# Transfers of adaLN rows two steps ahead of their products, through four buffers instead of two

## The chip, the cores and the metric

The kernel runs on one core of a Trainium2 chip. The metric is the time of one execution on the device in microseconds (us). Weights lie in the chip's main memory in 32-bit floats and are brought to the core by DMA, all of them started from one instruction queue, SyncE's (SP below). The matrix engine (PE), the vector engine (DVE), the scalar engine (ACT) and GpSimd (POOL) each work through a list of instructions of their own, in an order that is fixed when the kernel is built, and wait for one another by semaphores.

## What is computed

Two layers of a decoder trunk for 256 tokens of width 1024. A conditioning vector `c` gives six vectors per layer (shift, scale and gate of two sub-layers) by a product with a 1024 x 6144 matrix:

```python
c_act = jax.nn.silu(c)
for l in range(DEPTH):
    mod = c_act @ w_mod[l] + b_mod[l]
    sh1, sc1, g1, sh2, sc2, g2 = jnp.split(mod, 6, axis=-1)
    h = modulate(rms_norm(x, mix_norm_g[l]), sh1, sc1)
    y = token_mixer(h, ...)          # MLA, MoBA and a 31-tap convolution branch, gated and merged
    x = x + g1[:, None, :] * y
    h = modulate(rms_norm(x, ffn_norm_g[l]), sh2, sc2)
    x = x + g2[:, None, :] * channel_mixer(h, ...)
```

The change touches only how `mod` is made inside the token mixers.

## The kernel before

**Weights.** Every weight matrix comes as units of 128 x 1024 numbers (512 KB). `wload` (line 193) starts a transfer into a `raw` tile (four buffers); `split` (line 206) makes a high part `whi` with ACT (line 213) and the rest `wlo` with DVE (line 215), four buffers each; PE multiplies the activations by both (lines 291, 292 and 294). `take` keeps three units (`AHEAD`) split ahead of use.

**adaLN rows.** Part of `mod` is made on PE (`mod_part`, line 389) and part on DVE. On DVE, one step brings 128 x 1024 numbers of the transposed matrix (`in_wmr`, 512 KB), multiplies them by the broadcast row silu(c) (`crow`) and sums along the row in one instruction (`use_row`, line 372, the "row product" below; a short read of the sum comes with it), and a one-column addition of the bias follows (line 373). Each step gives one column of `mod`. In the token mixer of layer 0 there are 16 such steps (parts 3 and 4, eight each), in that of layer 1 there are 8 (part 2, the gate g1). `step "R"` (line 1185) does transfer and product in one step, by `mod_row`, with the buffers of the tag `qkT`, of which there are two. Sixteen more row products run in the channel mixer of layer 0, through other buffers (line 1252).

**The row silu(c).** The steps `RW` (`row_load`, line 1172) load `c` into a tile of the tag `kv` (two buffers), take its tanh with ACT into a tile of `qkT` (line 1181) and finish `crow` on DVE (line 1182). The other users of these tags in a mixer are earlier: `qkT` holds queries and keys of the two attentions, `kv` the keys and values of MLA, `vb` (one buffer, line 881) the values of MoBA, last read by PE in line 668.

**Order.** `CFG["order"]` lists each mixer's steps in the order in which they are written out; R steps are spread between the steps `r0` and `r1`. What an engine really does in which order is decided once, at build time, by the framework's scheduler: it walks through its own estimate of time and gives each engine, whenever the engine is free there, the ready instruction that was written first. A tile is given a buffer of its tag when one is free by the same estimate, and the instruction waits in place on the chip if that turns out too early. A row product can so stand far ahead of its place in the list, and short instructions that were written much later (the tables `ta` and `tb` of the next layer, line 487; the gain `gs` of the channel mixer, line 571) stand wherever nothing written earlier was ready.

**Around the rows in the mixers.** DVE also runs the convolution taps (line 1061), the gating of the attention output (`out_ab`, line 1121, which frees a PSUM bank of the tag `psb`, three in all), and the convolution's normalisation (lines 1071 to 1100): its sum of squares goes through DVE (line 497), POOL (line 498) and PE (line 527).

Of the kernel before, what the change touches and what calls it, by code (L numbers as in the profile page):

```python
# [9 lines left out]
F32 = mybir.dt.float32  # L10
# [7 lines left out]
P = 128  # L18
S = 256
NB = 2  # L20
# [22 lines left out]
CDMA = 1  # L43
# [11 lines left out]
LINE = 512  # L55
# [6 lines left out]
ROWS = [(0, 0), (0, 1), (1, 0), (1, 1)] + RPARTS  # L62
# [40 lines left out]
def _order(l):  # L103
    o = []
    for w in STEPS[l].split():
        name = w.rstrip("0123456789")
        o.append((name, *(int(d) for d in w[len(name):])))
    o = _spread(o, [("V", j, t, min(31, t + TAPS)) for j in range(4) for t in range(0, 31, TAPS)], ("v", 0), ("v", 1))
    if ("r", 0) in o:
        o = _spread(o, [("R", r, k) for n, r in RPARTS if n == l for k in range(KD)], ("r", 0), ("r", 1))  # L110
    o = _spread(o, [("M",)] * (9 * len(PARTS[l])), ("m", 0), ("m", 1))
    return [t for t in o if t[0].isupper() and not (l == 0 and C0K and t[:2] == ("C", 0))]


CFG = {"order": [_order(0), _order(1)]}
# [35 lines left out]
def trunk_kernel(ctx, tc, xT, crow, ccol, pos, invf, modb_d, cols_d, grow_d, wmh, wmr, wm, win1, wqkv,  # L151
# [6 lines left out]
    wk = ctx.enter_context(tc.tile_pool(name="wk", bufs=2))  # L158
# [4 lines left out]
    def nm(s):  # L163
        uid[0] += 1
        return f"{s}_{uid[0]}"
# [7 lines left out]
    def e1():  # L173
        return wk.tile([P, S], F32, tag="e1", name=nm("e1"), bufs=8)
# [14 lines left out]
    def small(n, tag="sm", bufs=12):  # L189
        return wk.tile([P, n], F32, tag=tag, name=nm(tag), bufs=bufs)  # L190


    def wload(src, tag="raw", bufs=4):
        n = src.shape[1]
        t = wk.tile([P, 1024], F32, tag=tag, name=nm("raw"), bufs=bufs, align_bytes=LINE if tag != "raw" else None)
        sy.dma_start(t[:, 0:n], src)
        return t[:, 0:n]


    SPARE = ("oah", "oal", "obh", "obl")  # L200
# [164 lines left out]
    mod = [per.tile([P, 48], F32, name=f"mod{l}") for l in range(L)]  # L365

    def wload_row(l, r, k, tag=None):
        return wload(wmr[ROWS.index((l, r)), k], tag or SPARE[(2 * k + r) % 4], 2 if tag else 1)

    def use_row(raw, row, l, r, k, scale):  # L370
        acc = small(1, "m0", 4)
        ve.scalar_tensor_tensor(raw, raw, scale, row, op0=ALU.mult, op1=ALU.mult, accum_out=acc)  # L372
        return ve.tensor_tensor(mod[l][:, r * 8 + k:r * 8 + k + 1], acc, modb[:, l, r * 8 + k:r * 8 + k + 1],
                                op=ALU.add)

    def mod_row(row, l, r, k, tag=None, scale=1.0):

        return use_row(wload_row(l, r, k, tag), row, l, r, k, scale)
# [53 lines left out]
    def step(gen, n=1):  # L432
        for _ in range(n):
            next(gen, None)
# [241 lines left out]
    crow1 = []  # L676
# [22 lines left out]
    def layer(l):  # L699
# [4 lines left out]
        if l == 0:  # L704
# [26 lines left out]
            def prepare_tile(k):  # L731
                n = 1 if k < 4 else 2
                raws0 = [wload_row(0, r, k) for r in range(n)]
                accs = small(2, "m0", 4)
                for r in range(n):
                    ve.scalar_tensor_tensor(raws0[r], raws0[r], 1.0, crow0[0], op0=ALU.mult, op1=ALU.mult,
                                            accum_out=accs[:, r:r + 1])
                mods0.append(ve.tensor_tensor(mod[0][:, 0:16].rearrange("p (r k) -> p k r", r=2)[:, k, 0:n],
                                              accs[:, 0:n],
                                              modb[:, 0, 0:16].rearrange("p (r k) -> p k r", r=2)[:, k, 0:n], op=ALU.add))  # L740
                if k >= 4:
                    g = small(1, "gs", 12)
                    ve.scalar_tensor_tensor(g, mod[0][:, 8 + k:9 + k], 1.0, cv(l, "mix_g")[:, k:k + 1],
                                            op0=ALU.add, op1=ALU.mult)
                    gains.append(g)
                with tc.issue_after(mods0[-1].ins) if k else ExitStack():
                    ve.tensor_tensor(xn[k // 4][:, k % 4, :], x[:, k, :], bcs, op=ALU.mult)
# [56 lines left out]
        for k in range(KD):  # L804
# [4 lines left out]
            t = e1()  # L809
# [68 lines left out]


        qks = [None, None]  # L880
        vb = wk.tile([P, NB, 512], F32, tag="vb", name=nm("vb"), bufs=1)

        pqkv = {}

# [274 lines left out]
        def attend(fn, g):  # L1159
            if (fn, g) not in attns:  # L1160
                attns[fn, g] = fn(g)
            step(attns[fn, g])

        run = {
            "KL": latents, "LE": lat_evac, "GLU": glu, "LR": lat_rstd, "LT": lat_T, "QKV": proj_qkv, "UQ": up_q, "UK": up_kv,
            "MS": mla_rstd, "MP": mla_prep, "BS": moba_rstd, "BP": moba_prep, "MA": lambda g, p: attend(mla_attn, g), "BA": lambda g, p: attend(moba_attn, g), "C": gate_c, "V": conv,
            "LN": conv_mean, "LS": conv_rstd, "LB": conv_silu, "G": gate_ab, "O": out_ab, "OC": out_c, "PR": project, "M": lambda: step(mods),
        }
# [13 lines left out]
                ve.scalar_tensor_tensor(crow1[0], th, 1.0, crow1[0], op0=ALU.add, op1=ALU.mult)  # L1182

        run["RW"] = row_load
        run["R"] = lambda r, k: mod_row(crow1[0], l, r, k, "qkT", 0.5 if CDMA else 1.0)
        for tok in CFG["order"][l]:
            run[tok[0]](*tok[1:])
        step(mods, 99)
# [87 lines left out]
    for l in range(L):  # L1276
        layer(l)
# [86 lines left out]
```

## Time and profile before

| | us |
|---|---|
| median of 3 runs | 927.59 (927.27 to 927.75) |
| the profiled execution, whole | 925.46 |
| its span in the trace | 923.2 |
| PE busy | 894.6 |
| DVE busy | 789.0 |
| ACT busy | 554.3 |
| row products on DVE (line 372), 40 | 48.7 |
| DVE idle before row products, for their DMA | 3.4 |

The span is what the trace covers; 2.3 us of the execution lie around it. An engine is busy while one of its instructions runs; matmuls overlap, so PE's busy time is not PE at its peak. "Idle before X, until Y" is the time in which an engine stood still ahead of instruction X, and Y is what ended the wait.

### The profile page before, as it was taken

The numbers are of one execution on the slowest core, as the hardware profiler recorded it, in microseconds if no ns is written. First come the engines' busy times: TensorE is split into PE (matmuls) and PEld (weight loads), VectorE is DVE, ScalarE is ACT, GpSimd is POOL, SyncE is SP. The second block draws the span as 40 slices with busy tenths as digits, with TensorE's granted clock in tenths as the row PEclk, the third lists the DMA queues.
The fourth block names the chain that finished last, engine by engine and source line by source line (L and its number), as shares of the span: only waits on it lengthen the run. The fifth ranks groups of instructions, "written<-read, shape, count | busy, mean of one in ns | idle before, by whom it ended". The sixth has DMA issues, their size and how long they took to land.

```text
span 923.2 us, 18669 instructions
## 1 busy us (share of the span) xinstructions
PE 894.6 (97%) x7327; PEld 839.7 (91%) x7327; DVE 789.0 (85%) x1530; ACT 554.3 (60%) x980; POOL 43.4 (5%) x32
## 2 busy tenths in 40 slices
PE   6999989989999999999999999999999999999998
PEld 5988878989997999999979988789999899999998
DVE  6989899999987899988964999999777798777774
ACT  4677588734754655566643675976465566556561
POOL 0011500000000000000000042000000000000000
PEclk7999999999998999999999999999999999999999
DMA  8956534599877788876743665538757766666641
GB/s 316 390 193 207 170 103 159 182 316 321 293 259 250 265 277 281 309 229 222 227 155 106 206 217 181 195 119 274 239 173 244 259 214 221 194 194 194 196 138 46
DMA packets 57975, 201.59 MB, mean 218 GB/s; under 512 B 6944, under 2 KB 8480, under 8 KB 57888
## 3 DMA queue, kind: packets, MB, share of 16 engines
q1 hardware_dynamic: 57888, 200.41, 65.2%
q8 instruction: 57, 0.93, 0.4%
q14 instruction: 30, 0.25, 0.1%
HBM read 199.33 MB, written 1.05 MB: 217 GB/s over the span
## 4 chain that ended last, share of the span: by engine, by line
PE 77%; DVE 10%; DMA 6%; ACT 3%; issue 2%; POOL 2%; SPq 0%; POOLq 0%; DVEq 0%; ACTq 0%
PE psb L291 15%; PE psb L292 15%; PE psb L294 15%; PE psa L292 7%; PE psa L291 7%; PE psa L294 7%; DVE wlo L215 3%; DMA raw<-in_wmr 2%; POOL rs L498 2%; PE psa L389 2%; DMA raw<-in_wup 1%; DVE cacc L1061 1%; PE psa L668 1%; PE psa L656 1%; DMA raw<-in_wmh 1%
## 5 line engine op out<-in xcount | busy, mean ns | idle before, releaser
L213 ACT ACTIVATE whi<-raw 128x1024 fp32r<-128x1024 f32 (+2 forms) x286 | 295.8, 1041 | 210.9 <-PE psb L292 86.5
L215 DVE TENSOR_TENSOR wlo<-raw,whi 128x1024 fp32r<-128x1024 f32 (+2 forms) x286 | 340.0, 1194 | 74.2 <-ACT whi L213 61.0
L291 PE MATMUL psb<-hh,whi 128*128 128x256 f32 x1088 | 261.2, 281 | 1.3 <-ACT thc L782 1.3
L292 PE MATMUL psb<-hl,whi 128*128 128x256 f32 x1088 | 258.3, 279 | 0.0
L291 PEld LDWEIGHTS psb<-hh,whi 128*128 128x128 f32 x1088 | 204.7, 188 | 8.3 <-issue 4.0
L292 PEld LDWEIGHTS psb<-hl,whi 128*128 128x128 f32 x1088 | 204.4, 188 | 1.2 <-DVE hl L565 0.5
L294 PE MATMUL psb<-hh,wlo 128*128 128x256 f32 x1088 | 148.5, 278 | 0.0
L294 PEld LDWEIGHTS psb<-hh,wlo 128*128 128x128 f32 x1088 | 135.0, 188 | 0.8 <-issue 0.8
L1061 DVE SCALAR_TENSOR_TENSOR cacc<-upad,cw,cacc 128x256 f32<-128x256 f32 x240 | 104.3, 476 | 0.1
L292 PE MATMUL psa<-mhl,whi 128*128 128x256 f32 x400 | 93.5, 277 | 0.2 <-DVE mhl L1143 0.2
L291 PE MATMUL psa<-mhl,whi 128*128 128x256 f32 x400 | 93.6, 277 | 0.0
L1240 DVE SCALAR_TENSOR_TENSOR e<-psb,fw,e 128x255 f32<-128x255 f32 (+1 forms) x176 | 83.7, 477 | 10.3 <-ACT e L1238 9.2
L292 PEld LDWEIGHTS psa<-mhl,whi 128*128 128x128 f32 x400 | 74.9, 188 | 0.4 <-DVE mhl L1143 0.4
L291 PEld LDWEIGHTS psa<-mhl,whi 128*128 128x128 f32 x400 | 74.9, 188 | 0.0
L498 POOL TENSOR_TENSOR rs<-rs,mhalf 128x16 f32<-128x16 f32 (+3 forms) x22 | 41.8, 1908 | 687.7 <-DVE rs L497 686.9
L1238 ACT ACTIVATE e<-psb,fb,fw 128x256 f32<-128x256 f32 x88 | 48.7, 553 | 28.1 <-DVE e L1240 15.8
L294 PE MATMUL psa<-mhl,wlo 128*128 128x256 f32 x400 | 53.6, 277 | 0.0
L372 DVE SCALAR_TENSOR_TENSOR raw<-raw,crow 128x1024 f32<-128x1024 f32 x40 | 48.7, 1218 | 3.6 <-DMA raw<-in_wmr 3.4
L294 PEld LDWEIGHTS psa<-mhl,wlo 128*128 128x128 f32 x400 | 49.2, 188 | 0.0
L291 PE MATMUL psb<-whi,hh 128*128 128x416 f32 (+1 forms) x96 | 31.7, 354 | 3.9 <-ACT hh L811 3.9
L1248 ACT ACTIVATE mhl<-e 128x256 fp32r<-128x256 f32 x44 | 18.3, 416 | 26.6 <-DVE e L1246 24.6
L389 PE MATMUL psa<-raw,cact 128*32 128x256 f32 x320 | 31.9, 432 | 0.6 <-DMA raw<-in_wm 0.6
(272 smaller groups left out, 1472.2 us busy)
## 6 DMA issues: line engine op xcount, KB each, us to landing
raw<-in_wup SPq DMA_DIRECT2D x88, 512.0 KB, 4.6
raw<-in_wmr SPq DMA_DIRECT2D x52, 512.0 KB, 5.2
raw<-in_wdn SPq DMA_DIRECT2D x44, 512.0 KB, 4.4
raw<-in_wm SPq DMA_DIRECT2D x40, 512.0 KB, 4.4
raw<-in_wgab SPq DMA_DIRECT2D x32, 512.0 KB, 4.9
raw<-in_wqkv SPq DMA_DIRECT2D x24, 512.0 KB, 4.8
raw<-in_win SPq DMA_DIRECT2D x16, 512.0 KB, 4.6
raw<-in_wgc SPq DMA_DIRECT2D x16, 512.0 KB, 4.4
```

The costliest lines, as they stand in the source:

```text
L213: ac.activation(hi, raw, AF.Copy)
L215: ve.tensor_tensor(lo, raw, hi.bitcast(F32), op=ALU.subtract)
L291: te.matmul(o, p1[0], p1[1], start=start, stop=False)
L292: te.matmul(o, p2[0], p2[1], start=False, stop=False)
L294: te.matmul(o, p3[0], p3[1], start=False, stop=stop)
L372: ve.scalar_tensor_tensor(raw, raw, scale, row, op0=ALU.mult, op1=ALU.mult, accum_out=acc)
L389: te.matmul(acc[32 * c:32 * c + 32, 0:S], cact[:, k:k + 1].to_broadcast([P, 32]), raw[:, c * S:(c + 1) * S], start=(k == 0), stop=(k == KD ...
L498: gp.tensor_tensor(r, r, mhalf[:, :n], op=ALU.pow)
L1061: ve.scalar_tensor_tensor(aj, upad[:, j, t:t + S], cw[:, j * 31 + t:j * 31 + t + 1], aj, op0=ALU.mult, op1=ALU.add)
L1238: ac.activation(t, src, AF.Identity, scale=fw[:, 2, c:c + 1], bias=fb[:, c:c + 1])
L1240: ve.scalar_tensor_tensor(t[:, d:S], src[:, 0:S - d], fw[:, 2 - d, c:c + 1], t[:, d:S], op0=ALU.mult, op1=ALU.add)
L1248: ac.activation(mh, th, AF.Copy)
```

## The change

A row step no longer starts its own transfer. The first R step of a mixer starts the transfers of rows 0, 1 and 2, and each later one that of the row two ahead of it, as long as there are any. Row n goes to a buffer of the tag `qkT`, `vb`, `qkT` or `kv`, in turn. The tile `vb` is now aligned to 512 bytes, as the other three are. The products, their number and the order of the steps in the list stay as they were, and so do the row products of the channel mixer.

```diff
     def wload_row(l, r, k, tag=None):
-        return wload(wmr[ROWS.index((l, r)), k], tag or SPARE[(2 * k + r) % 4], 2 if tag else 1)
+        return wload(wmr[ROWS.index((l, r)), k], *(tag or (SPARE[(2 * k + r) % 4], 1)))
...
-        vb = wk.tile([P, NB, 512], F32, tag="vb", name=nm("vb"), bufs=1)
+        vb = wk.tile([P, NB, 512], F32, tag="vb", name=nm("vb"), bufs=1, align_bytes=LINE)
...
-        run["R"] = lambda r, k: mod_row(crow1[0], l, r, k, "qkT", 0.5 if CDMA else 1.0)
+
+        coming_rows = [t[1:] for t in CFG["order"][l] if t[0] == "R"]
+        fetched = []
+
+        def fetch_row():
+            if coming_rows:
+                n = len(fetched)
+                fetched.append(wload_row(l, *coming_rows.pop(0), (("qkT", 2), ("vb", 1), ("qkT", 2), ("kv", 2))[n % 4]))
+
+        used = [0]
+
+        def row_step(r, k):
+            for _ in range(1 if fetched else 3):
+                fetch_row()
+            use_row(fetched[used[0]], crow1[0], l, r, k, 0.5 if CDMA else 1.0)
+            used[0] += 1
+
+        run["R"] = row_step
```

## Rows read from the trace of the kernel before

**Rows 1.** The page's first part: busy us, share of span, instructions.

```profile
PE 894.6 (97%) x7327; PEld 839.7 (91%) x7327; DVE 789.0 (85%) x1530; ACT 554.3 (60%) x980; POOL 43.4 (5%) x32
```

**Rows 2.** Busy us (instructions) per engine, PE clock, DMA share, GB/s; both row stretches.

```profile
181.00:262.00 81.00, 77.13 (x666) 74.34 (x659) 77.12 (x156) 41.18 (x61) 0.77 (x1) 1.00 0.90 312
...
614.00:657.00 43.00, 42.08 (x379) 40.77 (x377) 41.88 (x79) 28.02 (x55) 0.00 (x0) 1.00 0.75 255
```

**Rows 3.** Waits of the whole span: who waited for whom, us, times, longest.

```profile
DVE raw L372 <- DMA raw<-in_wmr: 3.4, 4, 1.6
...
SPq L196 <- DVE raw L372: 32.9, 21, 3.4
...
SPq L196 <- PE psa L601: 6.7, 1, 6.7
```

**Rows 4.** SP's timeline, layer 0's row transfers: start us, us, line, what.

```profile
156.77 0.33 SPq L196 DMA_DIRECT2D raw<-in_wmr  x1
...
184.72 0.33 SPq L196 DMA_DIRECT2D raw<-in_wmr  x1
```

**Rows 5.** DVE's timeline in layer 0's row stretch; idle before in brackets.

```profile
183.47 1.22 DVE L372 SCALAR_TENSOR_TENSOR raw<-raw,crow 128x1024 f32<-128x1024 f32 x1
...
184.61 1.22 DVE L215 TENSOR_TENSOR wlo<-raw,whi 128x1024 fp32r<-128x1024 f32 x1
...
186.15 0.15 DVE L373 TENSOR_TENSOR mod<-m,modb 128x1 f32<-128x1 f32 x1
...
191.20 1.23 DVE L372 SCALAR_TENSOR_TENSOR raw<-raw,crow 128x1024 f32<-128x1024 f32 x1 [1.57 <-DMA raw<-in_wmr]
...
192.35 0.68 DVE L1121 SCALAR_TENSOR_TENSOR b<-b,psb 128x512 f32<-128x512 f32 x1
...
206.68 0.22 DVE L487 TENSOR_TENSOR ta<-cs2a,grow 128x64 f32<-128x64 f32 x1
...
222.00 0.21 DVE L487 TENSOR_TENSOR ta<-cs2a,grow 128x64 f32<-128x64 f32 x1
...
224.89 1.23 DVE L372 SCALAR_TENSOR_TENSOR raw<-raw,crow 128x1024 f32<-128x1024 f32 x1 [1.08 <-DMA raw<-in_wmr]
...
228.06 0.15 DVE L497 TENSOR_SCALAR rs<-psb 128x2 f32<-128x2 f32 x1
```

**Rows 6.** PE's timeline, its two stops in the same stretch.

```profile
193.09 0.38 PE L291 MATMUL psb<-oah,whi 128*128 128x256 f32 x1 [2.41 <-DVE b L1121]
...
229.21 0.71 PE L527 MATMUL psb<-ident,rs 128*128 128x128 f32 x4 [1.42 <-POOL rs L498]
```

**Rows 7.** Instructions that read or write `grow` and `ta`, and the input of `gs`.

```profile
L357 SPq DMA_DIRECT2D grow<-in_grow x2: 405/414/423, 6.3 to 58.8; - x2
...
L1020 DVE TENSOR_TENSOR e<-ma,ta x8: 408/417/420, 95.7 to 552.6; 128x256 f32<-128x256 f32 x8
...
596.00 0.17 DVE L399 TENSOR_TENSOR mod<-psa,modb 128x8 f32<-128x8 f32 x1 [0.51 <-PE psa L397]
```

**Rows 8.** Timelines in layer 1's row stretch: DVE, and PE's stop.

```profile
624.42 0.16 DVE L571 SCALAR_TENSOR_TENSOR gs<-mod,col 128x8 f32<-128x8 f32 x1
...
626.63 1.23 DVE L372 SCALAR_TENSOR_TENSOR raw<-raw,crow 128x1024 f32<-128x1024 f32 x1 [0.61 <-DMA raw<-in_wmr]
...
638.58 0.68 DVE L672 TENSOR_TENSOR obl<-psa,obh 128x512 fp32r<-128x512 f32 x1
...
639.32 0.39 PE L292 MATMUL psb<-obl,whi 128*128 128x256 f32 x1 [0.92 <-DVE obl L672]
```

**Rows 9.** Layer 1: SP's row transfers and weights, PE's last reading of `vb`.

```profile
614.81 0.33 SPq L196 DMA_DIRECT2D raw<-in_wmr  x1
...
622.06 2.33 SPq L196 DMA_DIRECT2D raw<-in_wmr  x2
...
629.02 1.86 SPq L196 DMA_DIRECT2D raw<-in_wgab  x2
...
634.90 1.53 PE L668 MATMUL psa<-pT,vb 128*64 128x128 f32 x24
```

## The prediction

> **What bounds the kernel now.** I read the page's busy times first: PE is busy for 894.6 us of a span of 923.2 us, so 28.6 us is all that PE stands still anywhere [rows 1]. The change works in the two stretches in which the mixers' row products run, so the table by stretches came next [rows 2]. In layer 0 (181 to 262 us) PE is busy for 77.13 of 81.00 us and DVE for 77.12; in layer 1 (614 to 657 us) it is 42.08 and 41.88 of 43.00. PE and DVE are equally full there, at a granted PE clock of 1.00, so a DVE delay has little to hide behind, and at most 3.87 + 0.92 = 4.8 us can come back. Then the waits: DVE waited for row transfers 4 times, 3.4 us in all [rows 3]. Last, the engines' timelines around these four waits, to see which of them PE felt [rows 5, 6, 8].
>
> **What the change removes.** Before, the third row's transfer starts at 184.72, right behind the first product (183.47, some 1.2 us long) [rows 4, 5]: two buffers, so transfer n stands behind product n-2. SP waited 21 times and 32.9 us for row products, those of the channel mixer included [rows 3]. With four buffers transfer n stands behind product n-4, and the first four start before any product. I expect no wait of DVE for rows where these were:
> - 1.57 us ahead of the product at 191.20. Directly behind it stands line 1121 (192.35), which frees the bank for which PE stops 2.41 us until 193.09 [rows 5, 6]. All 1.57 us are on the path.
> - 1.08 us ahead of the product at 224.89. Line 497 (228.06) comes behind it, then POOL, then PE after a stop of 1.42 us at 229.21 [rows 5, 6]. With 1.57 us won before, PE and DVE both come that much earlier, and the further 1.08 us fit into the 1.42.
> - 0.61 us in layer 1 ahead of 626.63. DVE then has no other wait until line 672 (638.58), for which PE stops 0.92 us until 639.32 [rows 8]. All 0.61 us are on the path.
> - The rest of the 3.4 us (some 0.2 us, near 249) is followed by no stop of PE: nothing.
>
> Were this all, it would be 1.57 + 1.08 + 0.61 = 3.3 us.
>
> **What it moves.** The order on an engine is made by a scheduler that fills every open place with the earliest written instruction that is ready. Before, rows could not be ready, since their transfers hung on the buffers. Where such places were open can be read off DVE's order. A table `ta` of the next layer stands at 206.68, between two convolution taps [rows 5]. Its input came with a transfer issued at 58.8 us, and layer 0's readers of its buffer began at 95.7 us [rows 7]. It was written far behind all R steps, so it took the first place in about 100 us for which nothing better was ready. A loaded row would have had it. There are four such places with `ta` in this stretch, two near 207 and two near 222 (one row for each pair in [rows 5]). Up to the first of them six products stand in the order, and none can come earlier, because no later-written filler stands among them.
>
> With rows loaded, products go into these places and the later ones move up. A product occupies DVE for 184.61 - 183.47 = 1.14 us until the next instruction starts, and its bias addition is 0.15 us long and partly overlapped [rows 5], so 1.2 us a row. With k more rows ahead of line 497 than before, it and PE's stop at 229.21 move by 1.2 k - 2.65 us. The limits are k = 0 (-2.65), where a row once used does not come again, and k = 5 (+3.35), where all 16 rows stand ahead, since 11 already do. I take k = 2: the two places near 207 are certainly open, but rows put there delay the taps, and what becomes ready meanwhile was written before rows and takes the places near 222. So 2.4 - 2.65 = -0.25 us in layer 0. Ahead of 207 nothing changes but the wait. Behind 229 DVE has less to do and PE shows no stop until the stretch ends, so nothing more is won.
>
> In layer 1 the first such place is at 624.42, taken by `gs`, whose input was done at 596.00 [rows 7, 8]. Row 3 goes to a `kv` buffer that is free by then and fits there. It pushes line 672 by 1.2 us; with 0.61 us won, PE's stop grows from 0.92 to 1.5 us: +0.6 us. The bounds are -0.61 (no row comes forward) and 3 x 1.2 - 0.61 = +3.0: rows 1 and 5 go to `vb`, which PE still reads until 634.90 + 1.53 = 636.4 [rows 9], so of eight rows at most six stand ahead, and three do already. I take one, since there is one such filler.
>
> **DMA and SP.** The bytes are the same. The first four rows of layer 0 move ahead of 181 us, out of the fullest stretch (DMA share 0.90, 312 GB/s) [rows 2], which can only help; later ones start when products end, as now. Costed at nothing; the cover is the lead of four products in place of two. The alignment of `vb` adds no instruction; PE reads the same 24 pieces in 1.53 us [rows 9] from an address that is at most moved. Nothing.
>
> **Sum.** -0.25 + 0.6 = +0.35 us against the profiled execution's 925.46, so 925.8; the 2.3 us of it that lie around its span stay. The median of the runs, 927.59, stands 2.1 us above that execution, so I forecast 927.9.
>
> **Rivals.**
>
> (A) The forecast: waits go, products move forward and take the place of the waits; 927.9. Its own range has k = 1 to 3 and layer 1 from -0.6 to +0.6: 927.59 - 1.45 - 0.6 = 925.5 to 927.59 + 0.95 + 0.6 = 929.1.
>
> (B) Faster: the order ahead of lines 497 and 672 keeps its number of products and only the waits go: 927.59 - 3.3 = 924.3. For it: each wait has a stop of PE right behind it. Against it: the open places. The Trainium skill, "Perfetto Trace Analysis", section "Optimization Strategy", says that gaps which repeat on the engine that should be full can mean too few buffers for the next tile; by it this case would be the likeliest. The trace agrees in that SP waited for row products, but only four of 24 products were late.
>
> (C) Slower: DVE is full and more rows crowd in. With k = 4 in layer 0 (+2.15) and two rows in layer 1 (2 x 1.2 - 0.61 = +1.8) the time is 931.5. It decides from k = 3: beyond 2.65 / 1.2 = 2.2 rows each further one stops PE for its whole length, since line 497 is followed by POOL and PE at once [rows 5, 6]. For it: the two `ta` places near 222, still ahead of 228.06. Against it: only while the normalisation is unready do rows come first.
>
> (D) Slower by another way: in layer 1 row 1 goes to `vb`, which PE reads until 636.4. If its transfer stands in SP's list where row 1's stood (622.06), SP holds the weights behind it, those of 629.02 for 7 us. With three units split ahead, between none and all of that reaches PE; I take half: 931. Such a stop exists: SP waited 6.7 us for PE ahead of the row transfer at 614.81 [rows 3, 9]. Against it: the scheduler gives the buffer only when it thinks `vb` is free. The Trainium skill, "DMA: Bandwidth & Descriptors", section "Anatomy of one DMA — SWDGE (gpsimd) path", says that waits are made by the issuing sequencer and not by the DMA engines; by that a blocked row blocks all behind it, and the stop at 614.81 looks so.
>
> (E) Transfers do not come earlier, because SP reaches them behind weights that wait for DVE: 927.6.
>
> **How the numbers follow.** Chances: A 0.37, B 0.30, C 0.19, D 0.07, E 0.07. About 0.2% or 1.9 us is what a measurement can tell here. B is faster by 3.3 us, and the low edge of A (k = 1, no row in layer 1) is 2.1 us faster, so faster 0.31 with B's own failures taken out; C and D are slower, and A with k = 3 and two rows in layer 1 too: 0.29. The rest, 0.40, is no difference. The range goes from B with a little more (923.8) to C (931.8).
>
> **What would show it.** Right, step by step: no DVE idle before line 372 for row transfers; `ta` no longer alone near 207 but row products there, and the last row product of layer 0 well ahead of 249; PE's stop for line 1121 down from 2.41 to about 0.8 us; its stop ahead of line 527 grown from 1.42 to about 2.7 us (PE comes 1.57 us earlier, the normalisation 0.25), with 13 products ahead of line 497; its stop for line 672 about 1.5 us. Wrong if line 497 has as many products ahead of it as before (B), if DVE waits again for rows with four in flight, or if SP holds weights behind the transfer into `vb` (D). The forecast also fails if the scheduler reorders the stretch as a whole, so that other pairs of instructions meet.

## The result, and the profile after

| | before | after |
|---|---|---|
| median, us | 927.75 (925.2 to 933.5, 7 runs) | 923.88 (919.24 to 925.78, 7 runs) |
| the profiled execution, whole | 925.46 | 923.99 |
| its span | 923.2 | 922.1 |
| DVE idle before row products, for their DMA | 3.4 in 4 waits | 2.8 in 1 wait |

The ratio after / before is 0.9943, 95% interval 0.9917 to 0.9969: 5.3 us faster (2.9 to 7.7). I had forecast 927.9, no difference. The time lies inside my range, at its low edge, and close to that of rival B (924.3), whose order came true in layer 0 alone. The two spans differ by only 1.1 us, since the trace of after is 2.1 us behind that of before by 125 us already, ahead of any row transfer; part of that is its granted clock, 0.66 from 121 to 126 us where before had 1.00. So what follows compares stretches of the traces and not their spans.

The page's busy times of after, then the stretches of [rows 2] (columns as there):

```profile
PE 895.0 (97%) x7327; PEld 841.3 (91%) x7327; DVE 789.5 (86%) x1530; ACT 555.0 (60%) x980; POOL 43.3 (5%) x32
```

```profile
181.00:262.00 81.00, 79.09 (x684) 76.21 (x684) 78.94 (x159) 42.65 (x62) 0.78 (x1) 1.00 0.87 306
614.00:657.00 43.00, 43.00 (x393) 42.35 (x392) 38.00 (x68) 27.75 (x54) 0.00 (x0) 1.00 0.68 224
```

PE's work is the same, but it is busy for 2.0 us more of the first stretch and for all of the second. DVE has become emptier in layer 1 alone, 38.00 for 41.88 us. The waits of after that answer to [rows 3]:

```profile
DVE raw L372 <- DMA raw<-in_wmr: 2.8, 1, 2.8
...
SPq L196 <- DVE raw L372: 26.7, 18, 4.0
...
SPq L196 <- PE psa L668: 7.5, 1, 7.5
```

The last of these waits is in layer 0.

PE's timeline of after in layer 0's stretch has two stops. The one for line 1121 has shrunk from 2.41 us, the one ahead of line 527 [rows 6] is gone, and a new one stands ahead of line 1074. In layer 1's stretch there is none; the 0.92 us of [rows 8] are gone. This is one execution; the single stops change from one to the next, as the last sections show.

```profile
194.05 0.38 PE L291 MATMUL psb<-oah,whi 128*128 128x256 f32 x1 [0.76 <-DVE b L1121]
...
217.57 0.67 PE L1074 MATMUL psb<-e,mean_w 128*128 128x256 f32 x2 [1.14 <-DVE e L1073]
```

DVE's timeline of after, layer 0 (answers to [rows 5]):

```profile
192.17 1.22 DVE L372 SCALAR_TENSOR_TENSOR raw<-raw,crow 128x1024 f32<-128x1024 f32 x1
...
193.32 0.68 DVE L1121 SCALAR_TENSOR_TENSOR b<-b,psb 128x512 f32<-128x512 f32 x1
...
207.85 1.22 DVE L372 SCALAR_TENSOR_TENSOR raw<-raw,crow 128x1024 f32<-128x1024 f32 x1
...
215.86 1.22 DVE L372 SCALAR_TENSOR_TENSOR raw<-raw,crow 128x1024 f32<-128x1024 f32 x1
217.01 0.08 DVE L372 DVE_READ_ACCUMULATOR raw<-raw,crow 128x1 f32 x1
217.01 0.42 DVE L1073 TENSOR_TENSOR e<-e,e 128x256 f32<-128x256 f32 x1
...
227.87 0.15 DVE L497 TENSOR_SCALAR rs<-psb 128x2 f32<-128x2 f32 x1
```

No product waits for its DMA. One has taken the place of `ta` near 207, as forecast, and no table is left ahead of line 497 (five before: four of `ta`, one of `tb`). But the products ahead of line 497 are 11, exactly as before: only their places changed, from 7 to 8 ahead of line 1073 (217.01), with 8 ahead of line 1079 in both.

DVE's timeline of after, layer 1 (answers to [rows 8]), and SP's row transfers there (answers to [rows 9]):

```profile
621.85 1.22 DVE L372 SCALAR_TENSOR_TENSOR raw<-raw,crow 128x1024 f32<-128x1024 f32 x1
...
623.47 0.16 DVE L571 SCALAR_TENSOR_TENSOR gs<-mod,col 128x8 f32<-128x8 f32 x1
...
635.85 0.69 DVE L672 TENSOR_TENSOR obl<-psa,obh 128x512 fp32r<-128x512 f32 x1
...
643.17 1.23 DVE L372 SCALAR_TENSOR_TENSOR raw<-raw,crow 128x1024 f32<-128x1024 f32 x1 [2.78 <-DMA raw<-in_wmr]
```

```profile
599.33 0.42 SPq L196 DMA_DIRECT2D raw<-in_wmr  x1
...
613.84 0.33 SPq L196 DMA_DIRECT2D raw<-in_wmr  x1
...
621.10 2.34 SPq L196 DMA_DIRECT2D raw<-in_wmr  x2
...
636.34 0.38 SPq L196 DMA_DIRECT2D raw<-in_wmr  x1
```

The products moved back, not forward: one stands ahead of line 672 in place of three. Row 3, whose `kv` buffer is free early, is fetched first, at 599.33, row 0 at 613.84, rows 2 and 4 from 621.10 on; row 1, whose buffer is `vb`, follows at 636.34 when PE has done with `vb`. Its product at 643.17 waits 2.78 us, which stops PE nowhere, and rows 2, 3 and 4, long loaded, come only behind it.

### The profile page after: what moved, and what is told of

It is laid out like the page before. It is cut to its first block, busy times and chain, and to the rows that moved or that the text cites. A ratio compares the mean times of both kernels' runs of the same rounds, so it can differ in the third digit from the quotient of the medians.

```text
span 922.1 us, 18663 instructions
## 1 busy us (share of the span) xinstructions
PE 895.0 (97%) x7327; PEld 841.3 (91%) x7327; DVE 789.5 (86%) x1530; ACT 555.0 (60%) x980; POOL 43.3 (5%) x32
## 4 chain that ended last, share of the span: by engine, by line
PE 79%; DVE 9%; DMA 4%; ACT 4%; issue 2%; POOL 2%; SPq 0%; POOLq 0%; DVEq 0%; ACTq 0%
PE psb L291 16%; PE psb L292 16%; PE psb L294 15%; PE psa L291 7%; PE psa L292 7%; PE psa L294 7%; DVE wlo L215 3%; PE psa L389 2%; POOL rs L498 2%; DVE raw L736 1%; DMA raw<-in_wup 1%; PE psa L656 1%; ACT whi L213 1%; PE psa L668 1%; DVE cacc L1061 1%
```

## The experiments

Theory O: in layer 0 the gain is that of the waits, with the number of products ahead of PE's lines unchanged; in layer 1 it comes from the row in `vb`, which holds later products back. Each label below is one kernel of 7 to 12 runs. Executions of one and the same kernel scatter with a standard deviation of some 2.4 us, so the times resolve about 2 us. For what is finer I measured in each trace the time between two fixed matmuls of PE's list: from number 1259 to 1875 (186 to 262 us in before) and from 4712 to 5074 (618 to 660 us).

| kernel | time against before, us | layer 0 stretch | layer 1 stretch |
|---|---|---|---|
| before | | 75.97 | 42.02 |
| after | -5.3 (-7.7 to -2.9) | 73.41 | 40.75 |
| after once more | -6.4 (-8.5 to -4.3) | 73.89 | 40.96 |
| change in layer 0 alone | -3.1 (-5.0 to -1.1) | 72.87 | 42.04 |
| change in layer 1 alone | -1.7 (-3.7 to +0.4) | 76.23 | 40.70 |
| two buffers | +0.2 (-1.8 to +2.0) | 76.48 | 44.70 |
| no lead | -5.9 (-8.6 to -3.3) | 73.12 | 40.60 |
| own sums | -0.3 (-2.6 to +2.0) | 73.42 | 43.54 |
| no `vb` in layer 1 | -1.8 (-3.9 to +0.4) | 74.59 | 42.15 |
| before, held back in layer 1 | -3.2 (-4.9 to -1.4) | 76.72 | 41.05 |
| one later | -2.1 (-4.3 to +0.1) | 75.17 | 40.77 |
| three more | +5.1 (+3.0 to +7.2) | 83.65 | 40.77 |
| behind the mean | -3.4 (-5.6 to -1.4) | 72.96 | 40.74 |
| third too | -5.0 (-7.3 to -2.8) | 73.85 | 41.05 |

(The times are the ratio's distance from 1 times the median of before in the same runs.)

**Layer 0 alone.**

```diff
-        run["R"] = row_step
+        run["R"] = row_step if l == 0 else (lambda r, k: mod_row(crow1[0], l, r, k, ("qkT", 2), 0.5 if CDMA else 1.0))
```

> The change in layer 0's mixer alone; layer 1 keeps the kernel before (own transfer in each step, two buffers). Theory O (the waits go, and the order ahead of lines 497 and 1121 keeps its number of products): PE's stops at 193.09 (2.41 us) and 229.21 (1.42 us) shrink to one of about 0.8 for line 1121 and one of about 1.1 ahead of line 1074, so 3.83 - 1.9 = 1.9 us, up to the 2.65 us of DVE's two waits: 1.9 to 2.7 us faster than before. Layer 1 keeps its stop of 0.92 ahead of line 292. Rival theory V (the gain is layer 1's, from the products that the tile vb holds back there): about 0, within 0.5 us of before.

PE's timeline of this kernel; the third stop is layer 1's, unchanged:

```profile
192.95 0.39 PE L291 MATMUL psb<-oah,whi 128*128 128x256 f32 x1 [0.59 <-DVE b L1121]
...
216.07 0.67 PE L1074 MATMUL psb<-e,mean_w 128*128 128x256 f32 x2 [0.74 <-DVE e L1073]
...
637.37 0.38 PE L292 MATMUL psb<-obl,whi 128*128 128x256 f32 x1 [0.90 <-DVE obl L672]
```

3.1 us faster, with stops in layer 0 at the lines of after and that of before in layer 1. Theory V, all in layer 1, falls.

**Layer 1 alone** (the same with `l == 1`).

> The change in layer 1's mixer alone; layer 0 keeps the kernel before. Theory O with vb as the second cause: the stop of 0.92 us ahead of line 292 (for line 672) goes, since two products fewer stand ahead of line 672, and no DVE wait of 0.61 us stands there: 0.9 to 1.4 us faster than before; layer 0 keeps its stops of 2.41 and 1.42 us. Together with the run for layer 0 the two should make about the whole change's 4 to 5 us. Theory V: nearly all of the change, 4 us or more faster. My forecast before the result: 0.6 us slower.

```profile
193.50 0.38 PE L291 MATMUL psb<-oah,whi 128*128 128x256 f32 x1 [1.70 <-DVE b L1121]
229.27 0.71 PE L527 MATMUL psb<-ident,rs 128*128 128x128 f32 x4 [1.10 <-POOL rs L498]
...
634.63 0.39 PE L292 MATMUL psb<-obl,whi 128*128 128x256 f32 x1 [0.18 <-DVE obl L672]
```

PE's timeline has layer 0's two stops at the lines of before, if shorter, and only 0.18 us for line 672. The time, -1.7 us, doesn't exclude zero by itself; the stretch is 1.3 us shorter. The two halves add to -4.8.

**Two buffers, two steps ahead.**

```diff
-                fetched.append(wload_row(l, *coming_rows.pop(0), (("qkT", 2), ("vb", 1), ("qkT", 2), ("kv", 2))[n % 4]))
+                fetched.append(wload_row(l, *coming_rows.pop(0), ("qkT", 2)))
```

> Transfers are written two steps ahead, but with the two buffers of qkT alone. Theory O (the buffers do it; being written ahead is worth nothing where the buffer is not free): the order on DVE is that of before, DVE's four waits of 3.4 us in all and the stops of 2.41, 1.42 and 0.92 us stay: within 0.5 us of before. Rival theory S (it is the two steps of lead that bring the gain): as the whole change, 4 to 5 us faster.

```profile
DVE raw L372 <- DMA raw<-in_wmr: 4.1, 4, 1.4
```

The waits are those of before again (4, 3.4 us there), and the gain is gone. (From 614 to 657 us the granted clock of this trace was 0.96 and not 1.00, so its layer 1 stretch of 44.70 is left out below.)

**Four buffers, no lead.**

```diff
-            for _ in range(1 if fetched else 3):
+            for _ in range(1):
```

> Four buffers, but each step writes its own transfer, right ahead of its product as before. Theory O: as the whole change, 4 to 5 us faster, with the same order on DVE and stops of about 0.8 (line 291, for line 1121) and 1.1 us (line 1074) in layer 0 and none ahead of line 292 in layer 1. Theory S (the lead does it): within 1 us of before.

-5.9 us, with PE's stops 0.40 us (line 1121) and 1.19 us (line 1074) in layer 0 and none for line 672. So the four buffers bring the gain, and being written two steps ahead adds nothing that these times resolve; the two stretches are within 0.8 us of after's.

**After once more**, beside the next three.

> The changed kernel itself once more, for comparison with the three others on the same chip: 4 to 5 us faster than before if the first measurement (5.3 us, 2.9 to 7.7) holds; 3.3 us, what my steps gave for the waits alone, if the rest of it was scatter.

-6.4 us: the gain holds. Its interval excludes the 3.3 us of the waits alone.

**Own sums.** The sums of the products (line 371) get four tags in place of one of four buffers, so a loaded row may pass the one before it.

```diff
-        acc = small(1, "m0", 4)
+        acc = small(1, f"m0{k % 4}", 2)
```

> The changed kernel, with the sums of the row products in four tags of their own (by the number of the row in its part) in place of the one tag m0, so that a row that is loaded need not wait for the row before it, which lies in vb. In layer 1 four products then stand ahead of line 672 in place of one, which is the order that my forecast meant; layer 0 keeps the order of the change. Theory O with vb as the cause in layer 1: the stop for line 672 comes back with 0.92 + 1.2 - 0.61 = 1.5 us, so 1 to 2 us slower than the changed kernel and 0.6 us slower in layer 1 than before. Rival theory N (the order in layer 1 costs nothing, and layer 1 won only its 0.61 us of waiting): same as the changed kernel within 0.5 us.

PE's timeline of this kernel ahead of line 292, and DVE's around line 672:

```profile
635.59 0.38 PE L291 MATMUL psb<-obh,whi 128*128 128x256 f32 x1 [0.42 <-ACT obh L671]
...
638.52 0.38 PE L292 MATMUL psb<-obl,whi 128*128 128x256 f32 x1 [1.74 <-DVE obl L672]
```

```profile
634.71 1.22 DVE L372 SCALAR_TENSOR_TENSOR raw<-raw,crow 128x1024 f32<-128x1024 f32 x1
...
637.78 0.69 DVE L672 TENSOR_TENSOR obl<-psa,obh 128x512 fp32r<-128x512 f32 x1
```

Four products now stand ahead of line 672, which is the number that I had forecast, and PE's stop is 1.74 us where I had said 1.5. The stretch is 2.6 to 2.8 us longer than in after, and 1.5 longer than in before (+0.6 forecast). The time lies some 6 us above after's, more than the stretch explains; the intervals of the two leave room for that, but what else there may be is open. One part is seen here and in the next run: the granted clock from 725 to 740 us was 0.77 (0.89 in before and after), and matmuls 5074 to 5800 took 84.89 and 85.12 us (83.88 in before, 83.95 in after). That the order caused this is not shown.

**No `vb` in layer 1.** Rows go to `qkT`, `kv`, `qkT` there; the sums keep one tag.

```diff
-                fetched.append(wload_row(l, *coming_rows.pop(0), (("qkT", 2), ("vb", 1), ("qkT", 2), ("kv", 2))[n % 4]))
+                fetched.append(wload_row(l, *coming_rows.pop(0), ((("qkT", 2), ("vb", 1), ("qkT", 2), ("kv", 2))[n % 4] if l == 0 else (("qkT", 2), ("kv", 2), ("qkT", 2))[n % 3])))
```

> The changed kernel, but in layer 1 rows go to the two qkT buffers and one kv buffer alone, so no row waits for PE's last reading of vb; the row sums keep the one tag m0. Layer 0 is that of the changed kernel. Theory O (it was the row in vb that held the later products back, through the order of the sums): SP's wait of some 7.5 us for PE's line 668 goes, four products stand ahead of line 672 in place of one, its stop of PE comes back at 1.5 to 2 us, and the stretch from 618 to 660 us becomes 2.5 to 3 us longer than in the changed kernel, as in the run with four tags for the sums: the whole 1 to 4 us slower than the changed kernel. Rival theory M (the shared tag of the sums alone held them, vb plays no part): one product ahead of line 672 and the time of the changed kernel within 1 us.

```profile
637.94 0.38 PE L292 MATMUL psb<-obl,whi 128*128 128x256 f32 x1 [0.54 <-DVE obl L672]
...
646.06 0.67 PE L1074 MATMUL psb<-e,mean_w 128*128 128x256 f32 x2 [0.24 <-DVE e L1073]
```

Four products stand ahead of line 672 again (621.53 to 629.51), so theory M falls, and it takes both to hold them back: `vb` late, and sums given out in the order of the rows. The stretch is only 1.2 to 1.4 us longer than in the two profiles of after, and the stop for line 672 is 0.54 us in place of 1.74. All four lie well ahead of line 672 here and not, as in the run before, directly in front of it, which is likely why. One expectation failed: SP's wait of 7.5 us for line 668 is still there. It belongs to layer 0; the kernel with the change in layer 1 alone has none.

**Before, held back.** The two buffers of before; in layer 1 the products from the second on are held behind line 672 (`oblast` is that instruction; the lines that set it are left out).

```diff
...
-        run["R"] = lambda r, k: mod_row(crow1[0], l, r, k, "qkT", 0.5 if CDMA else 1.0)
+        def row_step(r, k):
+            with tc.issue_after(oblast[0].ins) if l == 1 and k > 0 else ExitStack():
+                mod_row(crow1[0], l, r, k, "qkT", 0.5 if CDMA else 1.0)
+
+        run["R"] = row_step
```

> The kernel before with its two buffers in both layers; only the row products of layer 1 from the second on are held behind the last line 672 by the scheduler, which gives DVE nearly the order that it has in the changed kernel there. Theory O: what layer 1 won came from the order, not from buffers: the stop of 0.92 us for line 672 goes and the time is 0.9 to 1.4 us below before. If layer 1 needs the buffers (rival): no gain, or slower by DVE waits for the held products.

```profile
614.00:657.00 43.00, 43.00 (x390) 42.25 (x390) 40.75 (x76) 28.18 (x54) 0.00 (x0) 1.00 0.79 257
```

With the order alone, and not one buffer more, PE is busy for all of layer 1's stretch, as in after; the stretch is 1.0 us shorter than in before. Layer 1's gain comes from products that stay out of the way. The time, -3.2 us, is more than that again.

**One later.** After, with layer 0's products from the seventh on held behind line 1073 (`zlast`; the lines that set it are left out), in `row_step`:

```diff
...
+            with tc.issue_after(zlast[0].ins) if l == 0 and used[0] >= 6 else ExitStack():
-            use_row(fetched[used[0]], crow1[0], l, r, k, 0.5 if CDMA else 1.0)
+                use_row(fetched[used[0]], crow1[0], l, r, k, 0.5 if CDMA else 1.0)
```

> The changed kernel, with layer 0's row products from the seventh on held behind line 1073 by the scheduler. In the changed kernel one product stands in the place of ta near 207 and delays line 1073, for which PE stops 1.14 us ahead of line 1074. Here ta stands there again, two products stand between lines 1073 and 1079, and ten in place of eleven ahead of line 497. Theory O (each product ahead of a line that PE waits for costs its 1.2 us): the stop of 1.14 us goes, 0.6 to 1.1 us faster than the changed kernel. Rival: the two products behind line 1073 delay line 1079 and with it line 497 as much, and a stop ahead of line 527 comes back: same within 0.5 us.

```profile
224.66 0.58 PE L519 MATMUL psb<-ones,e 128*128 128x1 f32 x4 [0.97 <-DVE mod L373]
...
239.71 0.39 PE L291 MATMUL psb<-uh,whi 128*128 128x256 f32 x1 [0.38 <-ACT b L1110]
...
241.75 0.38 PE L292 MATMUL psb<-ul,whi 128*128 128x256 f32 x1 [0.48 <-DVE ul L1100]
```

The stop ahead of line 1074 is gone and others stand behind it; the stretch is 1.3 to 1.8 us longer than in the two profiles of after. What matters more: I had expected ten products ahead of line 497. Six stand ahead of line 1073, but again 8 ahead of line 1079 and 11 ahead of line 497. The products that were pushed out of one place came back in the next.

**Three more.** Layer 0's first thirteen row steps are put into the list directly ahead of the step that squares the convolution (`LS`), with `_early` standing for that reordering:

```diff
-CFG = {"order": [_order(0), _order(1)]}
+CFG = {"order": [_early(_order(0)), _order(1)]}
```

> The changed kernel, but the first thirteen row products of layer 0 are written ahead of the step that makes the convolution's sum of squares, so that the scheduler must prefer them: 14 in place of 11 stand ahead of line 497, 8 as before ahead of lines 1073 and 1079. This is my forecast's move with k = 3. Theory O (a product ahead of line 497 costs its 1.2 us, less what PE comes late): 3 x 1.2 = 3.6 us less the some 0.6 to 0.9 us by which POOL's result now lies ahead of PE's reading in line 527, so 2.7 to 3.0 us slower than the changed kernel in this stretch, 2 us faster than before in all; a stop of 2 to 3 us ahead of line 527. Rival theory N (DVE has that much room, so the number of products ahead is free): same as the changed kernel within 0.5 us.

PE's timeline and the table by stretches (columns as in [rows 2]):

```profile
231.78 1.08 PE L389 MATMUL psa<-raw,cact 128*32 128x256 f32 x8 [3.20 <-DMA raw<-in_wm]
...
235.81 1.22 PE L527 MATMUL psb<-ident,rs 128*128 128x128 f32 x4 [2.01 <-POOL rs L498]
```

```profile
220.00:232.00 12.00, 8.80 (x77) 8.58 (x80) 12.00 (x23) 5.39 (x7) 0.00 (x0) 0.94 1.01 386
...
230.00:231.00 1.00, 0.00 (x0) 0.00 (x0) 1.00 (x3) 0.00 (x0) 0.00 (x0) 0.79 1.02 418
231.00:232.00 1.00, 0.22 (x4) 0.20 (x8) 1.00 (x2) 0.00 (x0) 0.00 (x0) 0.50 1.02 328
232.00:240.00 8.00, 5.99 (x31) 5.12 (x24) 5.54 (x16) 1.09 (x2) 1.59 (x1) 0.50 0.60 198
```

Theory N, that the number is free, falls: with 14 products ahead of line 497 DVE is full (12.00 of 12.00 us), the line comes at 233.84 in place of 227.87, and the stretch is 10 us longer than in after. But it is no clean measure of my price of 1.2 us a product. Two more weight splits (line 215, 1.1 us each) stand ahead of line 497 too (15 in place of 13). The stop ahead of line 527 is there (2.01 us). The larger stop of 3.20 us is for a weight: in this order PE uses `in_wm` ahead of line 519, where in after it comes at 235.91, and the transfer, issued at 225.73, is late while the DMA engines are full. The granted clock falls during the larger stop and stays at 0.50 until past 240, some 10 us, which costs up to 5 us more. What a further product alone costs there stays open.

**Behind the mean**, and **third too.** After, with layer 0's products from the eighth on held behind the last line 1079 (`mlast`); in the second kernel the third product also behind line 1121 (`olast[1]`).

```diff
...
+            with ExitStack() as stack:
+                if l == 0 and used[0] == 2:
+                    stack.enter_context(tc.issue_after(olast[1].ins))
+                if l == 0 and used[0] >= 7:
+                    stack.enter_context(tc.issue_after(mlast[0].ins))
-            use_row(fetched[used[0]], crow1[0], l, r, k, 0.5 if CDMA else 1.0)
+                use_row(fetched[used[0]], crow1[0], l, r, k, 0.5 if CDMA else 1.0)
```

(The first kernel lacks the lines with `olast`; those that set `mlast` and `olast` are left out.)

> The changed kernel, with layer 0's row products from the eighth on held behind the last line 1079, so that none stands between lines 1072 and 1079; tables of the next layer (0.2 us each) take the place, and ten in place of eleven products stand ahead of line 497. Theory O: the stop ahead of line 1074 (0 to 1.2 us in the runs so far) goes and no line that PE waits for comes later, unlike in the run that held them behind line 1073 only: 0.4 to 1.1 us faster than the changed kernel. Rival (as in that run, the order as a whole is worse where it is touched): 2 to 4 us slower than the changed kernel.

> As the run before it, and in addition layer 0's third row product is held behind line 1121 ahead of which it stands (PE stops 0.4 to 1.3 us for that line 1121 in the changed kernel); three short tables take its place there. Theory O: that stop shrinks by 1.2 - 0.6 us too: 0.8 to 1.7 us faster than the changed kernel, with PE's stop for line 1121 under 0.3 us. Rival: the held product delays a later line as much, same as the run before it or slower.

The first kernel's stop behind the place that was cleared:

```profile
224.71 0.58 PE L519 MATMUL psb<-ones,e 128*128 128x1 f32 x4 [0.84 <-DVE mod L373]
```

In both 10 products stand ahead of line 497, as I expected. The stop ahead of line 1074 goes, and one of 0.84 and 1.07 us ahead of line 519 takes its place. Line 1121 still stops PE for 0.59 and 0.83 us, the second against what I expected. Neither is faster than after: -3.4 and -5.0 us where after made -5.3 and -6.4. No version that I tried beats it.

## Why the prediction was wrong

**The waits go: right.** I had priced 1.57 + 1.08 = 2.65 us in layer 0. The six profiles with after's order there have a stretch of 73.55 us on average (72.87 to 74.59), the four with before's 76.35 (75.97 to 76.72): 2.8 us. PE's stops up to line 527 add up to 1.0 to 2.3 us in the six and to 2.8 to 4.6 in the four; a stop ahead of line 527 is in all four and in none of the six. Single stops say less. The one for line 1121 was 2.41 us and is 0.76 in after, where I had said 0.8, but it is 0.12 to 1.83 in the five others of that order and 1.32 to 1.70 in the three others of before's; so the hit on that number is luck.

In layer 0 two buffers were too few, though only four products were late in all: the run with two buffers (+0.2 us) and the run with four and no lead (-5.9 us) show that it is the number of buffers. In layer 1 their number was not the cause: "before, held back" has the shorter stretch with two. The Trainium skill's rule on gaps that repeat ("Perfetto Trace Analysis", section "Optimization Strategy"), which I set against the forecast under rival B, named the right cause for layer 0, and only there.

**A term that I left out.** That 2.8 us come out so near 2.65 is luck in part. My term 1.2 k - 2.65 counts products alone, and a table that gives up its place takes its own time along. DVE from its first product to line 497, in before and in after (columns as in [rows 2]):

```profile
183.47:228.06 44.59, 41.91 (x365) 40.35 (x363) 41.64 (x82) 19.54 (x25) 0.00 (x0) 1.00 0.90 314
```

```profile
185.45:227.87 42.42, 40.52 (x354) 39.13 (x353) 40.91 (x77) 18.60 (x23) 0.00 (x0) 1.00 0.89 322
```

DVE's work there is 0.73 us shorter (41.64 and 40.91), as the five tables of 0.21 to 0.29 us went behind line 497. The 2.65 us of waits for rows are gone, and 1.2 us more of waits for ACT's high parts (line 213) have come in their place. On average over the four and the six profiles it is 2.4 us of waits and 0.8 us of work less, and 0.4 us of waits for ACT more. No run separates what the tables are worth to PE from what the waits are.

**k = 2 in layer 0: this step failed.** I counted the places of the tables as room, put products there, and concluded that two more would stand ahead of line 497. A product did go to 207.85, as the step said. The number ahead of line 497 stayed 11, so there was nothing to set against the waits: layer 0 gained 2.8 us where I had -0.25. I had the bound k = 0 in the text and set it aside. What the runs show in its place: a product that comes early is missing later (7 and 8 ahead of lines 1073 and 1079 became 8 and 8), and those held back behind line 1073 come again ("one later": 6, 8 and 11); only those held behind line 1079 stay away (7 and 10 in the last two kernels). Why the number stays 11 is open. That the scheduler had no more idle time of DVE to give ahead of line 497, whatever was loaded, is how I read it; its estimate was not looked at.

**A stop that I had not seen.** In after PE stops 1.14 us ahead of line 1074. That the product which moved ahead of line 1073 makes this stop is not shown: it is in four of the six profiles of that order (0.74 to 1.19 us), but not in "after once more", and two of the four with before's order have it too (0.87 us in "two buffers", 0.86 in "held back"). It is absent in the three kernels that hold products behind that place.

**Layer 1: this step had the wrong sign.** I let row 3 take the place of `gs` (+0.6 us). The rows in `vb` I only counted as two that could not come forward. I overlooked that the sums share one tag and are given out in the order of the rows, so that row 1 holds back rows 2 to 4. `gs` kept its place (623.47), two products fewer stood ahead of line 672, and the stop of 0.92 us went (0 to 0.21 us in the profiles of that order): the stretch is 1.2 us shorter (eight profiles of 40.60 to 41.05 against 42.02 and 42.04). That products which come forward there cost time was right: in the two runs that let them the stretch is up to 1.4 and 2.8 us longer than in after.

**DMA and SP, rival D.** SP does stand still for PE's last reading of `vb`, 7.5 us, but in layer 0, which I had not considered, and it costs nothing: the weight behind it follows at 173.24 where before it was issued at 171.33, and PE was 1.9 to 2.1 us later there already, in an order that had not changed. PE reaches matmul 1259 at 186.9 to 188.5 us in the ten profiles with this transfer and at 186.1 to 188.5 in the four without. In layer 1 the transfer into `vb` stands behind the weights (636.34), as the argument against D had it.

**The sum** with the two failed terms replaced is 927.59 - 2.65 - 1.2 = 923.7; the median is 923.88, nearer than the scatter allows to count. The shortened stretches make 2.8 + 1.2 = 4.0 us. The times of after, of after once more and of "no lead", which has the same order, are 5.3, 6.4 and 5.9 us; each interval alone reaches down to 4.3 or less, but all three lie above 4.0. Where one or two microseconds more would come from stays open. No other part of PE's list is shorter throughout: from matmul 1875 to 4712 the three took 354.70 to 355.15 us, the four kernels with before's layer 0 351.65 to 356.01, and behind 5074 264.2 us against 263.1 to 265.3.

## What to carry to other kernels

Where a fixed order is packed by a scheduler, more buffers take waits away, but they need not bring more work forward: before pricing work that "could move", count what stands ahead of the line that the bounding engine waits for, short fillers included. Here the number of products stayed at 11 in layer 0, while five fillers left, and went from 3 to 1 in layer 1. Look for everything that keeps the order of the pieces (a shared result tag, one late buffer in a rotation): a late piece holds back the loaded ones behind it, for better or worse. A buffer count and a prefetch distance are two changes; try each alone. And where whole times scatter by more than the effect, compare the time between two fixed instructions, in more than one trace.

## What the runs showed of the hardware

TensorE's granted clock can fall in the middle of a dense stretch: in "three more" it was 0.79 from 230 to 231 us and 0.50, the lower of its levels (1.2 GHz), from 231 to 240. It fell while PE stood still for 3.20 us, until 231.78, and was low already when PE stopped again for 2.01 us, until 235.81. In before, stops of 2.41 and 1.42 us [rows 6] left it at 1.00 [rows 2]. So a stop can cost more than its length. In that kernel DMA moved 386 GB/s at a share of 1.01 from 220 to 232 us, and the late weight shows in PE's longest stop.
